# Gather of the experts' inputs one group ahead, sums in fixed bunches, and the norm's factors behind the gather

## Chip, cores and metric

One NeuronCore of a Trainium2 chip runs the whole program. The metric is the device time of one execution in microseconds. TensorE is written PE, VectorE DVE, ScalarE ACT, GpSimd POOL, and SyncE, which issues the loads, SP.

## What is computed

Three layers act on 512 tokens of 1024 numbers in float32: a hybrid layer, then two layers of a mixer followed by a mixture of experts. The change is in the two mixtures and in the norm before each:

```python
x = _layer_norm(DEEPNORM_ALPHA * x + mix, ln_g[i, 0], ln_b[i, 0])
ffn = _hierarchical_moe(x, ...)      # router: 4 groups, 8 experts each, top 2
x = _layer_norm(DEEPNORM_ALPHA * x + ffn, ln_g[i, 1], ln_b[i, 1])

def expert_block(xb, e):             # xb: the rows routed to expert e
    h = jax.nn.silu(xb @ w_gate[e]) * (xb @ w_up[e])
    return h @ w_down[e]
y = jax.ops.segment_sum(y_rows * row_gate[:, None], row_tok, num_segments=t + 1)[:t]
```

There are 32 experts with a hidden width of 512. The first mixer is a state-space scan (SSD), the second a dilated attention.

## The kernel before

The hybrid layer runs to about 1.3 ms, the SSD mixer to 1805 us. Then come the experts of layer 0, the attention, and the experts of layer 1.

**Experts (`moe`, from L2291).** Every expert has 64 slots; what does not fit goes to `moe_overflow`, a loop that runs zero times here. Two experts make a pair and lie side by side in PE's 128 columns: `experts_up` (L2127) and `experts_down` (L2160) issue each weight matmul as 64 columns at `tile_position=(0, 64 * u)`, `u` being the expert of the pair. 16 pairs run one after the other; the down matmuls of pair c - 1 stand behind the up matmuls of pair c. The weights are float32 and streamed: 6.29 MB an expert, 201.3 MB a layer, in 192 pieces of 1.05 MB, each of two loads of 512 KB from SP's queue (`mload`, L2097). A piece is the four k steps of one of gate or up for one expert, or half of its down matrix. 11 buffers hold pieces (seven slots with the halves `rawa` and `rawb`, two `mrawp`, two `mraw`), and 11 pieces are asked for before the stage begins.

**Gather (`gather`, L2253).** For four experts (a group, two pairs) a one-hot `OH` of 256 slots picks the tokens: 64 matmuls of `X` (the normed input in a high and a low part, `hl`, four token tiles `t`, eight feature blocks `k`) make `XG`. It is done for a group right before that group's first pair, the second half of it inside that pair (`yield` after k = 3). Its PSUM banks `acc`, two of them, are shared with the sums. ACT and DVE take turns in emptying them (L2274, L2276).

**Sums (`combine`, L2187).** For each token tile and half of the features, `cmb` adds the slots' outputs `yy` back by a one-hot `sel`, and DVE adds the bank into `x`. `Fill` deals these out, three steps behind the up matmuls and three behind the down matmuls of a pair. The last group is 32 matmuls behind the last weight.

**Route (`route_with`, L1930, to `moe_gates`).** While the mixer's output projection (`g_out`, L305) makes token tile t, the tile before it is transposed (`tp`), copied (`xt`, ACT and DVE in turn), multiplied with the router weights (`pl`), and DVE picks group and two experts in a dozen small instructions (L1970 to L1982, one-hots `oh`, their sum `O`). Then `ln_apply` or `ln_apply3` normalises `x`. In `moe`, ACT casts `x` to the high part of `X` and POOL subtracts to get the low part (L2327, L2328). `moe_slots` (L2004) turns all four `O` into slot numbers `pos` in one group of matmuls `pp`, which needs the last tile; the first one-hot, the first gather and the first weight matmul follow.

**What sets the order.** The program is written as one stream; a scheduler moves instructions on each engine by its own estimates of when operands and buffers come free, so the order on an engine differs from the order written.

## Time and profile before

| | |
|---|---|
| time, median of 3 runs | 3299.06 us (3298.2 to 3310.43) |
| the profiled execution: its time, its span | 3303.4 us, 3301.6 us |
| mean granted clock of PE | 0.970 |
| PE busy | 3130.1 us (95%), 15183 matmul records |
| DVE, ACT, POOL busy | 1484.8, 998.4, 736.9 us |
| DMA | 603.43 MB, mean 183 GB/s |

A row of a timeline has start, duration, engine, line, operation, output and inputs by name, tile sizes and the number of records that were joined; in brackets stands the idle time before it and what ended it. A float32 matmul leaves two records, one of a split (fp32r) operand one. In the waits, "A <- B: total, times, longest" is time in which A had nothing to do until B ended; SPq is the queue of loads. [...]

### The profile page before, as it was taken

What the parts mean: (1) busy time and instruction counts of PE and PEld (TensorE: products, weight loads), DVE (VectorE), ACT (ScalarE), POOL (GpSimd) and SP (SyncE); (2) the same over time, 40 slices, a digit from 0 to 9 for tenths busy, and PEclk for the clock granted to TensorE, in tenths of its full rate; (3) what the DMA queues carried; (4) which work ended last, traced back from release to release, by engine and by line L of the source; (5) the groups of instructions that cost most, each with busy time, mean ns of one, the idle gap of its engine ahead of it and who ended that gap; (6) DMA issues with size and microseconds to landing.
All of it is one profiled execution on the core that took longest, in us unless ns stands there. A gap on an engine that the chain in (4) does not pass through costs nothing. (4 is left out here: it accounts for less than half of the span.)

```text
span 3301.6 us, 40067 instructions
## 1 busy us (share of the span) xinstructions
PE 3130.1 (95%) x15183; PEld 2166.0 (66%) x15183; DVE 1484.8 (45%) x3035; ACT 998.4 (30%) x1866; POOL 736.9 (22%) x560
## 2 busy tenths in 40 slices
PE   8899998999999999999998899999999988999997
PEld 6678787887877888777877544444488874444443
DVE  5655766533244313488767322222444464222223
ACT  4434666642232223244423100000234431000011
POOL 3442323422342222123224100000164321000000
PEclk9999999999998999999999899999999988999999
DMA  5624121225342323233434799999822237999996
GB/s 164 139 91 114 41 65 38 82 86 161 120 138 64 102 90 94 66 103 99 118 93 153 286 388 358 361 363 355 313 65 64 65 105 291 392 357 363 366 350 250
DMA packets 294433, 603.43 MB, mean 183 GB/s; under 512 B 29392, under 2 KB 154764, under 8 KB 294204
## 3 DMA queue, kind: packets, MB, share of 16 engines
q1 hardware_dynamic: 294236, 600.82, 52.5%
q8 instruction: 122, 2.00, 0.2%
q14 instruction: 75, 0.61, 0.1%
HBM read 587.04 MB, written 13.70 MB: 182 GB/s over the span
## 5 line engine op out<-in xcount | busy, mean ns | idle before, releaser
L333 POOL TENSOR_TENSOR lob<-rawb,whi 128x1024 fp32r<-128x1024 f32 (+1 forms) x57 | 151.5, 2660 | 779.0 <-ACTq L2214 538.4
L352 PE MATMUL lin<-hT,whi 128*128 128x512 f32 (+1 forms) x912 | 302.5, 411 | 22.3 <-ACT g L538 13.8
L2134 PE MATMUL mm<-rawb,XG 128*64 128x512 f32 x704 | 262.1, 600 | 0.0
L263 PE MATMUL mm<-hT,whi 128*128 128x512 f32 x832 | 260.1, 394 | 0.0
L2134 PE MATMUL mm<-rawa,XG 128*64 128x512 f32 x704 | 259.1, 599 | 0.0
L243 DVE TENSOR_TENSOR loa<-rawa,whi 128x1024 fp32r<-128x1024 f32 (+2 forms) x90 | 111.9, 1243 | 281.5 <-ACT whi L242 280.1
L243 POOL TENSOR_TENSOR lob<-rawb,whi 128x1024 fp32r<-128x1024 f32 x52 | 131.8, 2535 | 411.5 <-ACT whi L242 367.3
L352 PEld LDWEIGHTS lin<-hT,whi 128*128 128x128 f32 (+1 forms) x912 | 174.5, 194 | 69.1 <-ACT g L538 15.1
L242 ACT ACTIVATE whi<-rawa 128x1024 fp32r<-128x1024 f32 (+2 forms) x90 | 90.4, 1004 | 348.1 <-issue 184.3
L2269 PEld LDWEIGHTS xg<-OH,X 128*128 128x128 f32 x1024 | 132.0, 194 | 78.1 <-issue 74.6
L263 PEld LDWEIGHTS mm<-hT,whi 128*128 128x128 f32 x832 | 157.1, 189 | 38.0 <-ACT hT L439 0.2
L2197 PE MATMUL cmb<-yy,sel 128*128 128x512 f32 x512 | 155.7, 427 | 11.8 <-ACT yy L2177 2.9
L352 PE MATMUL lin<-xT,whi 128*128 128x512 f32 x512 | 165.2, 400 | 0.0
L2197 PEld LDWEIGHTS cmb<-yy,sel 128*128 128x128 f32 x512 | 90.8, 192 | 108.6 <-issue 57.1
L2269 PE MATMUL xg<-OH,X 128*128 128x256 f32 x1024 | 152.1, 296 | 2.7 <-DVE OH L2259 2.7
L390 POOL TENSOR_TENSOR ln<-lnv,mhalf 128x1 f32<-128x1 f32 x16 | 13.4, 840 | 603.7 <-DVE lnv L388 600.2
L263 PE MATMUL mm<-xT,whi 128*128 128x512 f32 (+1 forms) x400 | 129.9, 405 | 1.2 <-ACT xT L439 1.2
L2171 PE MATMUL py<-rawa,H 128*64 128x512 f32 x288 | 129.9, 598 | 0.0
L2134 PEld LDWEIGHTS mm<-rawa,XG 128*64 128x64 f32 x704 | 70.3, 136 | 90.3 <-issue 84.3
L369 PE MATMUL lin<-whi,hT 128*128 128x256 f32 x640 | 126.1, 289 | 1.7 <-ACT gv L992 1.1
L2171 PE MATMUL py<-rawb,H 128*64 128x512 f32 x288 | 127.4, 598 | 0.0
L333 DVE TENSOR_TENSOR loa<-rawa,whi 128x1024 fp32r<-128x1024 f32 (+1 forms) x55 | 73.9, 1344 | 110.2 <-ACT whi L332 103.2
(609 smaller groups left out, 7166.2 us busy)
## 6 DMA issues: line engine op xcount, KB each, us to landing
rawa<-in_moe_w_up_dram SPq DMA_DIRECT2D x92, 512.0 KB, 8.8
rawb<-in_moe_w_up_dram SPq DMA_DIRECT2D x92, 512.0 KB, 10.1
rawa<-in_moe_w_gate_dram SPq DMA_DIRECT2D x84, 512.0 KB, 8.3
rawb<-in_moe_w_gate_dram SPq DMA_DIRECT2D x84, 512.0 KB, 9.7
rawa<-in_moe_w_down_dram SPq DMA_DIRECT2D x72, 512.0 KB, 9.4
rawb<-in_moe_w_down_dram SPq DMA_DIRECT2D x72, 512.0 KB, 10.1
mrawp<-in_moe_w_down_dram SPq DMA_DIRECT2D x60, 512.0 KB, 10.1
mraw<-in_moe_w_gate_dram SPq DMA_DIRECT2D x52, 512.0 KB, 9.1
```

What stands on the lines that cost most here:

```text
L242: nc.scalar.activation(h, t[:, :, :o], AF.Copy)
L243: (self.second if j else nc.vector).tensor_tensor(lo[:, :, :o], t[:, :, :o], h, op=OP.subtract)
L263: nc.tensor.matmul(ps[j][:m], lhsT=w[:, k, 128 * j:128 * j + m], rhs=v, start=(kc + k == 0 and i == 0), stop=(kc + k == K - 1 and i == 2))
L333: (nc.gpsimd if j or self.late > 0 else nc.vector).tensor_tensor(lo, t, h, op=OP.subtract)
L352: nc.tensor.matmul(ps[:m], lhsT=w[:, k, 128 * j:128 * j + m], rhs=v, start=(k == 0 and i == 0), stop=(k == 7 and i == 2))
L369: nc.tensor.matmul(ps[:, :width], lhsT=v[:, 128 * t:128 * t + 128], rhs=w[:, k, :width], start=(k == 0 and i == 0), stop=(k == 7 and i == 2))
L390: self.nc.gpsimd.tensor_tensor(r, v, self.half[:, :n], op=OP.pow)
L2134: nc.tensor.matmul(ps[64 * u:64 * u + 64], lhsT=XG(4 * h + k, u), rhs=w[u][k], start=(h == k == 0), stop=(h == 1 and k == 3), skip_group_c ...
L2171: nc.tensor.matmul(py[c][s], lhsT=H[:, 2 * h + k, s], rhs=w[u][2 * k + c], start=(h == k == 0), stop=(h == k == 1), skip_group_check=True, ...
L2197: nc.tensor.matmul(ps, lhsT=sel[rows, 128 * t:128 * t + 128], rhs=yy[rows, hl, s], start=(n == 0), stop=(n == 2 * len(group) - 1))
L2269: nc.tensor.matmul(s, lhsT=X2[t][:, hl, k], rhs=OH[:, t], start=(hl == t == 0), stop=(hl == 1 and t == 3))
```

## The change

- The norm before the experts is split. The gather takes (x - mean) x r, made by ACT with a stride (`lny`), cast by ACT and subtracted by DVE; the gain and bias are applied by ACT when a gathered block is emptied (`gathered`), eight instructions of 256 columns for a group. The norm of `x` itself (`norm_in`) is done on DVE during the first pair.
- Slots, positions and the first one-hots are made for each token tile (`tile_slots`), and the first gather (`gather0`) goes by token tile into four `mm` banks.
- Later gathers are made one group ahead. Gather steps and sums stand in `between`, called behind each of gate, up and down, and are dealt out at four of six such places in two pairs.
- In a pair the expert `u` = 1 comes first.
- The sums of pair 14 are a group of their own, so the last group is 16 matmuls. The rows of gain and bias for the last norm are loaded ahead of the last down matmuls.
- `xT`, `hT` and `X` lie in four more fixed slots; the router's weights are padded from 36 to 40 columns; `moe_setup` loads gain and bias once more in columns (four small loads).

```diff
 class Block2:
-    def ln_apply3(self, p, x, t, stats, g, b, y):
-        m = p.tile([128, 1], F, name="lnmr", bufs=4)
-        nc.gpsimd.tensor_tensor(m, nm, r, op=OP.mult)
-        nc.scalar.activation(y, x[:, t], AF.Identity, bias=m, scale=r)
-        nc.vector.tensor_tensor(y, y, g, op=OP.mult)
-        nc.gpsimd.tensor_tensor(x[:, t], y, b, op=OP.add)
...
     def route_with(self, units, x, i, sums, p, xt, junk, y):
+        self.X2 = [self.in_slot(f"X{i}_{t}", self.SLOTS + t, [128, 2, 8, 128], R) for t in range(4)]
...
             if n % 2 == 0 and n:
-                self.route_tile(x, i, n // 2 - 1, pl, st, p, rows, y)
+                self.route_tile(x, i, n // 2 - 1, pl, p, y)
+                if n > 2:
+                    self.tile_slots(n // 2 - 2, pl)
         self.router_half(x, i, 7, xt, pl)
-        self.route_tile(x, i, 3, pl, st, p, rows, y)
+        self.tile_slots(2, pl)
+        self.route_tile(x, i, 3, pl, p, y)
+        self.tile_slots(3, pl)
         self.moe_gates(p)
...
-        (nc.scalar.activation(v, ps.rearrange("p (k t) -> p k t", k=4), AF.Copy) if h
-         else nc.vector.tensor_copy(v, ps.rearrange("p (k t) -> p k t", k=4)))
+        nc.scalar.activation(v, ps.rearrange("p (k t) -> p k t", k=4), AF.Copy)
...
-        if t == 2:
-            self.ln_apply3(p, x, t, st[t], rows[:, 0], rows[:, 1], y[:, t % 2])
-        else:
-            self.ln_apply(x, t, st[t], rows[:, 0], rows[:, 1], y[:, t % 2])
+        m = p.tile([128, 1], F, name="lnmr", bufs=4)
+        tt(m, nm, r, op=OP.mult)
+        X, z = self.X2[t], y[:, t % 2].rearrange("p (k f) -> p k f", k=8)
+        nc.scalar.activation(z, x[:, t].rearrange("p (f k) -> p k f", k=8), AF.Identity, bias=m, scale=r)
+        nc.scalar.activation(X[:, 0], z, AF.Copy)
+        tt(X[:, 1], z, X[:, 0], op=OP.subtract)
+
+    def tile_slots(self, t, pl):
+        pp = pl[t][:, 64:96]
+        for u in range(t + 1):
+            nc.tensor.matmul(pp, lhsT=self.lt16[:, 0 if u == t else 1], rhs=self.O[:, u], start=(u == 0), stop=(u == t),
+                             skip_group_check=True)
+        nc.vector.scalar_tensor_tensor(self.pos[:, t], pp, 1.0, self.O[:, t], op0=OP.add, op1=OP.mult)
+        self.one_hot(t, 0)
...
     def experts_up(self, piece, XG, n=2, between=lambda: None):
...
                 for k in range(4):
-                    for u in range(n):
+                    for u in reversed(range(n)):
                         nc.tensor.matmul(ps[64 * u:64 * u + 64], lhsT=XG(4 * h + k, u), rhs=w[u][k],
...
-                if which == h == 0:
-                    between()
+            between()
...
-    def experts_down(self, piece, H, gate, n=2):
+    def experts_down(self, piece, H, gate, n=2, between=lambda: None):
...
-                    for u in range(n):
+                    for u in reversed(range(n)):
...
+        between()
         yy = self.myy.tile([128, 2, D], R, name="yy")
...
+    def gather0(self, i):
+        xg = self.mq.tile([128, 8, 256], F, name="XG", bufs=2)
+        ps = [self.mm() for _ in range(4)]
+        s = lambda k: ps[k // 2][:, 256 * (k % 2):256 * (k % 2) + 256]
+        for t in range(4):
+            for k in range(8):
+                for hl in range(2):
+                    nc.tensor.matmul(s(k), lhsT=self.X2[t][:, hl, k], rhs=self.OH[:, t], start=(t == hl == 0),
+                                     stop=(t == 3 and hl == 1), skip_group_check=True)
+        for k in range(8):
+            self.gathered(i, xg, k, s(k))
+        return xg
+
+    def gathered(self, i, xg, k, ps):
+        self.nc.scalar.activation(xg[:, k], ps, AF.Identity, bias=self.gcol[:, i, 1, k:k + 1], scale=self.gcol[:, i, 0, k:k + 1])
+
+    def gather(self, i, e, out):
...
-            if k % 2:
-                o = xg[:, k - 1:k + 1].rearrange("p k s -> p (k s)")
-                if k % 4 == 1:
-                    nc.scalar.activation(o, ps, AF.Copy)
-                else:
-                    nc.vector.tensor_copy(o, ps)
-            if k == 3:
-                yield xg
+            self.gathered(i, xg, k, s)
+            yield
+        self.slot_values(e)
+        yield
...
+    def norm_in(self, x, i):
+        rows, y = (self.myy.tile([128, 2, D], F, name=n, tag="yy") for n in ("lnin", "lniny"))
+        for n, v in enumerate(("ln_g_2", "ln_b_2")):
+            self.bc_row(rows[:, n], self.a[v][i, 0])
+        for t in range(4):
+            self.ln_apply(x, t, (self.lnst2[:, t, 0:1], self.lnst2[:, t, 1:2]), rows[:, 0], rows[:, 1], y[:, t % 2])
+            yield
...
-                for t in range(4):
-                    xv = x[:, t].rearrange("p (f k) -> p k f", k=8)
-                    nc.scalar.activation(X2[t][:, 0], xv, AF.Copy)
-                    nc.gpsimd.tensor_tensor(X2[t][:, 1], xv, X2[t][:, 0], op=OP.subtract)
-                self.moe_slots(r, p)
...
+                XG = {0: self.gather0(i)}
...
+                def between():
+                    n = beat[0] = beat[0] + 1
+                    if n == 1:
+                        self.slot_values(0)
+                        self.norm_start()
+                    if n < 5:
+                        nq.step(1)
+                        gq.step((1, 3, 2, 3)[n - 1])
+                    elif (n - 5) % 6 in (0, 2, 3, 5):
+                        gq.step(1)
+                        cq.step(2)
+                        gq.step(2)
...
                         if c % 2 == 0:
-                            rest = self.gather(2 * c, X2)
-                            XG = next(rest)
+                            gq.flush()
+                            if c < 14:
+                                gq.add(self.gather(i, 2 * c + 4, XG))
...
-                    elif c and c % 2 == 0:
-                        fill.add(self.combine(x, group, self.ALPHA if c == 2 else 1.0))
+                    elif c and (c % 2 == 0 or c == 15):
+                        cq.add(self.combine(x, group, self.ALPHA if c == 2 else 1.0))
                         group = []
```

**PE, in the middle of layer 0's experts.** `mm` are up matmuls, `py0` and `py1` down matmuls of the two halves of the features, `cmb` sums, `xg` the gather. Slot numbers stand behind `rawa` and `rawb`: of slots 2 and 3, 1 and 2 or 3 and 4 one holds a piece of the one expert and one of the other. Before:

```order
L2171 MATMUL py1_14944<-rawb_1_77,H_14871 64x512
L2134 MATMUL mm_15050<-rawa_3_87,XG_15013 64x512
L2134 MATMUL mm_15050<-rawa_2_81,XG_15013 64x512
L2134 MATMUL mm_15050<-rawa_3_87,XG_15013 64x512
L2134 MATMUL mm_15050<-rawb_2_83,XG_15013 64x512
L2197 MATMUL cmb_15273<-yy_14971,sel_14976 128x512
L2197 MATMUL cmb_15279<-yy_14971,sel_14976 128x512
L2197 MATMUL cmb_15273<-yy_14971,sel_14976 128x512
L2197 MATMUL cmb_15279<-yy_14971,sel_14976 128x512
L2134 MATMUL mm_15050<-rawb_3_89,XG_15013 64x512
L2134 MATMUL mm_15050<-rawb_2_83,XG_15013 64x512
L2134 MATMUL mm_15050<-rawb_3_89,XG_15013 64x512
```

With the change, the same stage:

```order
L2186 MATMUL py1_15189<-rawb_2_83,H_15097 64x512
L2186 MATMUL py1_15189<-rawb_1_77,H_15097 64x512
L2213 MATMUL cmb_15338<-yy_15256,sel_15261 128x512 x2
L2213 MATMUL cmb_15344<-yy_15256,sel_15261 128x512
L2150 MATMUL mm_15275<-rawa_4_93,XG_14805 64x512
L2150 MATMUL mm_15275<-rawa_3_87,XG_14805 64x512
L2150 MATMUL mm_15275<-rawa_4_93,XG_14805 64x512
L2150 MATMUL mm_15275<-rawa_3_87,XG_14805 64x512
L2213 MATMUL cmb_15344<-yy_15256,sel_15261 128x512
L2304 MATMUL xg_15350<-OHr_13622,X0_0_13626 128x256
L2304 MATMUL xg_15350<-OHr_13622,X0_1_13627 128x256
L2304 MATMUL xg_15350<-OHr_13622,X0_2_13628 128x256
```

Before, the stretch ends behind one matmul of `rawb_2`, whose partner in `rawb_3` comes behind four sums. With the change the stretches between other work hold an even number from the two slots in turn, and single gather blocks and sums stand between them.

**PE, from the last projection to the first gather, layer 0.** `tp` are transposes of `x`, `pl` the router's matmuls (and with the change the slots of one tile), `pp` the slots of all tiles. Before:

```order
L1959 MATMUL pl<-wr_7981,xt 128x36 x4
L1954 MATMUL tp<-c_61,x_7968 128x128 x4
L1959 MATMUL pl<-wr_7981,xt 128x36 x8
L2013 LDWEIGHTS lt_8032
L2013 MATMUL pp<-O,lt_8032 128x32
```

With the change:

```order
L1970 MATMUL pl<-wr_7978,xt 128x40 x4
L1966 MATMUL tp<-c_61,x_7965 128x128 x4
L2279 MATMUL mm<-OHr,X_0_13626 128x256 x9
L2007 LDWEIGHTS lt_8036
L2007 MATMUL pl<-O,lt_8036 128x32
L2279 MATMUL mm<-OHr,X_0_13626 128x256 x7
L2007 LDWEIGHTS lt_8036
L2007 MATMUL pl<-O,lt_8036 128x32
```

Before, the ten matmuls and the four of `pp` follow the last `pl`, and all 64 of the gather come behind them (32 of these behind the first weights). With the change the 16 gather matmuls of tile 0 stand ahead of the last two `pl`, and those of tiles 1 and 2 between the slots of later tiles.

**POOL before and DVE after, in the route of layer 0.** `X` is the low part of the gather's input. POOL before:

```order
L2328 TENSOR_TENSOR X_14000<-x_7968,X_14000 128x1024
L390 TENSOR_TENSOR ln<-lnv,mhalf 128x1
L1369 TENSOR_TENSOR lnmr<-lnm,ln 128x1
L2328 TENSOR_TENSOR X_14004<-x_7968,X_14004 128x1024
L1372 TENSOR_TENSOR x_7968<-lny,lnrows 128x1024
L2031 CAST val<-c_61 128x128
L2037 CAST val_14053<-c_61 128x4 x4
L390 TENSOR_TENSOR ln<-lnv,mhalf 128x1
```

DVE with the change:

```order
L1995 TENSOR_TENSOR lnmr<-lnst 128x1
L1989 MAX m_8026<-rw 128x8
L1990 MAX_INDEX rix<-m_8026,rw 128x8
L1562 SCALAR_TENSOR_TENSOR x_7965,lnsum<-x_7965,mm 128x512
L1991 TENSOR_TENSOR oh<-c_61,rix 128x64
L1993 TENSOR_TENSOR O<-oh 128x32
L1999 TENSOR_TENSOR X_2_13628<-lny,X_2_13628 128x1024
L1982 SCALAR_TENSOR_TENSOR rw<-br_7982,lnst,pl 128x40
L2009 SCALAR_TENSOR_TENSOR pos<-pl,O 128x32
L1983 SCALAR_TENSOR_TENSOR rL<-rw,lnst,br_7982 128x40
L2014 TENSOR_TENSOR OHr<-c_61,pos 128x256
```

The four subtracts of 128x1024 have gone from POOL to DVE, where they stand between the routes of two tiles; the slots and the one-hot of a tile stand among the instructions of the next.

## Rows read from the trace of the kernel before

**Rows 1.** Windows: us; busy PE, PEld, DVE, ACT, POOL; PEclk, DMA share, GB/s.

```profile
1820.00:1840.00 20.00, 12.39 (x74) 10.24 (x75) 11.16 (x41) 2.95 (x4) 6.20 (x10) 0.65 0.05 14
1850.00:2350.00 500.00, 493.89 (x2218) 216.99 (x2216) 120.30 (x255) 45.59 (x73) 0.00 (x0) 1.00 0.97 372
1860.00:1880.00 20.00, 20.00 (x114) 9.80 (x112) 3.39 (x5) 3.65 (x6) 0.00 (x0) 1.00 1.03 413
2320.00:2340.00 20.00, 19.65 (x80) 8.12 (x79) 5.53 (x8) 1.97 (x3) 0.00 (x0) 1.00 1.03 410
2800.00:3200.00 400.00, 395.30 (x1752) 173.38 (x1749) 93.46 (x194) 35.72 (x57) 0.00 (x0) 1.00 0.96 370
```

**Rows 2.** Waits, expert stage of layer 0: total us, times, longest.

```profile
PEld mm L2134 <- DMA rawb<-in_moe_w_down_dram: 1.3, 4, 0.4
...
SPq L2097 <- PE mm L2134: 138.4, 109, 7.9
SPq L2097 <- PE py L2171: 66.5, 35, 7.2
```

**Rows 3.** PE's timeline in layer 0: start, us, engine, line, operation, tiles, records.

```profile
2137.90 1.94 PE L2134 MATMUL mm<-mraw,XG 128*64 128x512 f32 x8
2139.77 1.80 PE L2269 MATMUL xg<-OH,X 128*128 128x256 f32 x13
...
2145.86 1.93 PE L2171 MATMUL py<-rawa,H 128*64 128x512 f32 x4
2147.72 0.97 PE L2197 MATMUL cmb<-yy,sel 128*128 128x512 f32 x3
...
2165.12 1.07 PE L2134 MATMUL mm<-mrawp,XG 128*64 128x512 f32 x2
```

**Rows 4.** PE's timeline from the last projection to the first weight, layer 0.

```profile
1804.30 0.40 PE L305 MATMUL mm<-whi,ssd_yl 128*128 128x512 f32 x1
...
1814.73 3.63 PE L1959 MATMUL pl<-wr,xt 128*128 128x36 f32 x16 [5.94 <-DVE xt L1957]
...
1826.49 0.18 PE L2013 MATMUL pp<-O,lt 128*128 128x32 bf16 x1 [5.08 <-DVE O L1982]
...
1828.18 6.74 PE L2269 MATMUL xg<-OH,X 128*128 128x256 f32 x32 [1.39 <-DVE OH L2259]
...
1835.64 1.94 PE L2134 MATMUL mm<-rawa,XG 128*64 128x512 f32 x8
```

**Rows 5.** The timelines of DVE, then POOL, then ACT, same stretch.

```profile
1806.81 5.17 DVE L1981 TENSOR_TENSOR oh<-c,rix 128x32 f32<-128x32 f32 x2
...
1812.66 1.28 DVE L1361 SCALAR_TENSOR_TENSOR lny<-x,lnm,lnrows 128x1024 f32<-128x1024 f32 x1
...
1823.29 2.72 DVE L1997 TENSOR_TENSOR rex<-m 128x4 f32<-128x4 f32 x1
...
1827.62 1.77 DVE L2259 TENSOR_TENSOR OH<-c,pos 128x256 fp32r<-128x256 f32 x4
...
1806.79 2.85 POOL L2328 TENSOR_TENSOR X<-x,X 128x1024 fp32r<-128x1024 f32 x1 [3.36 <-DVE x L1569]
...
1823.14 2.85 POOL L2328 TENSOR_TENSOR X<-x,X 128x1024 fp32r<-128x1024 f32 x1 [3.79 <-ACT X L2327]
...
1804.61 2.10 ACT L2327 ACTIVATE X<-x 128x1024 fp32r<-128x1024 f32 x1
```

**Rows 6.** PE's timeline from the last projection to the first weight, layer 1.

```profile
2719.96 0.40 PE L305 MATMUL mm<-whi,mol 128*128 128x512 f32 x1
...
2745.28 1.94 PE L2134 MATMUL mm<-rawa,XG 128*64 128x512 f32 x8
```

**Rows 7.** PE's timeline at the end of layer 0's experts.

```profile
2377.20 2.13 PE L2197 MATMUL cmb<-yy,sel 128*128 128x512 f32 x8 [0.68 <-DVE x L2201]
```

**Rows 8.** ACT's timeline, layer 0's route and first gather.

```profile
1822.97 0.20 ACT L1995 ACTIVATE rg<-rg 128x16 f32<-128x16 f32 x1
...
1832.69 0.60 ACT L2274 ACTIVATE XG<-xg 128x512 f32<-128x512 f32 x1 [6.45 <-PE xg L2269]
```

More of the change, by code (lines that the diff above doesn't have):

```diff
@@ L1246, in block1 @@
         with ExitStack() as s1:
-            hp = self.pool(s1, "hT")
-            hT = [hp.tile([128, 8, 512], R, name=f"hT{i}") for i in range(2)]
+            hT = self.stage_in("hT")
             x = lambda k: (hT[0][:, k], hT[1][:, k])
@@ L1344, with ln_stats @@
     ALPHA = 4.0 ** 0.25
-    def ln_stats(self, p, x, t, sums, j):
+    def ln_stats(self, p, x, t, sums, j, out=(None, None)):
         nc = self.nc
-        nm = p.tile([128, 1], F, name="lnm", bufs=4)
+        nm = p.tile([128, 1], F, name="lnm", bufs=4) if out[0] is None else out[0]
         nc.vector.tensor_tensor(nm, sums[:, 0:1], sums[:, 1:2], op=OP.add)
@@ L1598, in ssd @@
                 fill.flush()
-            rows = q.tile([128, 2, D], F, name="lnrows", tag="xsT")
-            for n, v in enumerate((a["ln_g_2"][0, 0], a["ln_b_2"][0, 0])):
-                self.bc_row(rows[:, n], v)
             finish(3, y)
+            s1.close()
+            self.route_begin()
             xt = q.tile([128, 4, 512], F, name="xt", tag="xsT")
@@ L1606, in ssd @@
                             lambda t: q.tile([128, D], BF, name="lnj", tag="zt", bufs=1),
-                            rows, lny)
+                            lny)
 class Attn:
@@ L1644, in att_begin @@
     def att_begin(self, st):
-        xp = self.pool(st, "xT3")
-        self.xT = [xp.tile([128, 8, 512], R, name=f"xT{i}") for i in range(2)]
+        self.xT = self.stage_in("xTa")
         self.ap0 = self.pool(st, "att0", bufs=2)
@@ L1756, in att @@
                             lambda t: p2.tile([128, D], BF, name="lnj", tag="sS", bufs=4),
-                            rows, lny)
+                            lny)
     def att_qk(self, g, w, xx, cos, sin):
@@ L1919, in moe_setup @@
+                nc.vector.tensor_tensor(br[:, 1], br[:, 1], ps[:, 40:80], op=OP.add)
                 self.routers.append((wr, br))
         self.rL = p.tile([128, 4, 40], F, name="rL")
-        nc.gpsimd.memset(self.rL[:, :, 4:8], BIG)
         self.m8 = p.tile([128, 2, 4, 8], F, name="m8")
-        self.oh = [p.tile([128, 4, 32], F, name=f"oh{k}") for k in range(2)]
+        self.ohs = p.tile([128, 4, 2, 32], F, name="oh")
+        self.oh = [self.ohs[:, :, k] for k in range(2)]
         self.O = p.tile([128, 4, 32], BF, name="O")
@@ L1925, in moe_setup @@
         self.gate = [p.tile([128, 4], F, name=f"gate{k}") for k in range(2)]
+        self.gcol = p.tile([128, 2, 2, 8], F, name="gcol")
+        for i in range(2):
+            for n, v in enumerate(("ln_g_2", "ln_b_2")):
+                nc.sync.dma_start(self.gcol[:, i, n], a[v][i, 0].rearrange("(p k) -> p k", k=8))
         self.lt16 = p.tile([128, 2, 128], BF, name="lt16")
@@ L1928, in moe_setup, with route_begin, route_with @@
         nc.gpsimd.memset(self.lt16[:, 1], 1.0)
-    def route_with(self, units, x, i, sums, p, xt, junk, rows, y):
-        pl, v, st = {}, {}, {}
+    def route_begin(self):
+        self.rst = ExitStack()
+        p = self.pool(self.rst, "route", side="right")
+        self.pos = p.tile([128, 4, 32], F, name="pos")
+        self.OH = p.tile([128, 4, 256], R, name="OHr")
+        self.lnst = p.tile([128, 4, 2], F, name="lnst")
+    def route_with(self, units, x, i, sums, p, xt, junk, y):
+        self.X2 = [self.in_slot(f"X{i}_{t}", self.SLOTS + t, [128, 2, 8, 128], R) for t in range(4)]
+        pl = {}
         for n, _ in enumerate(units):
@@ L2002, in moe_gates @@
         nc.vector.tensor_tensor(g1, g0, ex, op=OP.mult)
-    def moe_slots(self, p, keep):
-        nc = self.nc
-        tt, stt = nc.vector.tensor_tensor, nc.vector.scalar_tensor_tensor
-        O, pos = self.O, self.pos
-        lt, one = self.lt16[:, 0], self.lt16[:, 1]
-        pp = self.acc("pp")
-        for t in range(4):
-            for u in range(t + 1):
-                nc.tensor.matmul(pp[:, 32 * t:32 * t + 32], lhsT=lt if u == t else one, rhs=O[:, u],
-                                 start=(u == 0), stop=(u == t))
-        for t in range(4):
-            nc.tensor.matmul(pp[:, 128:160], lhsT=one, rhs=O[:, t], start=(t == 0), stop=(t == 3))
-        stt(pos, pp[:, 0:128].rearrange("p (t e) -> p t e", t=4), 1.0, O, op0=OP.add, op1=OP.mult)
-        nc.vector.tensor_scalar(pos, pos, 1.0, None, op0=OP.subtract)
-        nc.vector.tensor_copy(self.cnt, pp[:, 128:160])
     def moe_values(self, p, keep):
@@ L2058, in moe_spill @@
         tt(st, end, nb, op=OP.subtract)
[L2059 removed]
+        ts(st, st, 64.0, -65.0, op0=OP.mult, op1=OP.add)
         far = 65536.0
```

161 lines of the change are left out of this document (86 added, 75 removed).

## Prediction

> **What bounds the kernel now.** I read the windows first, then the waits, then the timeline of TensorE (PE). In the two expert stages, which are 1060 of the 3301.6 us, PE is busy 99% of the time at full clock and the weight stream moves 372 and 370 GB/s, against 410 to 413 in its busiest stretches [rows 1]. The waits say who waits for whom: over 500 us PE waits 1.3 us for a weight, and the load queue (SPq) waits 138.4 and 66.5 us for buffers that PE has still to free [rows 2]. So PE sets the pace there, and the stream has some 10% in hand.
>
> What PE does with its time is in the timeline. A weight matmul fills 64 of the 128 columns, and each f32 instruction leaves two records. Eight records on alternating halves, four instructions, take 1.94 us; four records of one half, two instructions, take 1.93; one instruction by itself takes 1.07 [rows 3]. So an instruction holds its half for 1.93 - 1.07 = 0.86 us, and two on different halves overlap fully: with a partner it costs 0.43 us, and 0.86 if its partner comes only after other work.
>
> Between the mixers and the first weight matmul lies a second kind of time, PE idle. In layer 0 the last output-projection matmul starts at 1804.30 and the first weight matmul at 1835.64; between them PE waits 5.94 us for `xt` and 5.08 us for `O`, both from VectorE (DVE) [rows 4]. In that stretch PE runs the 32 gather matmuls in 6.74 us, with a mean granted clock of 0.65 [rows 1, 4]. DVE is late for small things: two 32-wide compares last 5.17 us and a 4-wide subtract 2.72 us, each while a 2.85 us subtract (or the add behind it) holds GpSimd (POOL) [rows 5]. In layer 1 the same path takes 25 us [rows 6].
>
> **Part 1: the order of the experts' matmuls.** I counted along PE's order, in the stretches of weight matmuls between other work, how many instructions have no partner on the other half: 74 of 768 in layer 0 and 76 in layer 1 before; 0 and 2 in the changed order. The reversed `u` does this, together with the bunches. Terms per layer: 74 x 0.43 = -31.8 us. Of the first group's gather 32 matmuls move out of the stage into the route; 13 of them take 1.80 us, so 32 take 4.4: -4.4. Of the sums 8 to 12 more matmuls fall before the last weight; three take 0.97 and eight 2.13 us [rows 3, 7], so 0.23 each and 0.27 for a start: +2.3. The sums stand in 8 to 11 more stretches: +2.5. Weight stretches fall only from 110 to 104 and 102, so the scheduler does not keep the "four bunches" as written: about -1, and gather stretches +1. The sum is -31.4. Walking the whole order with such prices gives 525 us before (measured 531) and 498 after in layer 0, 526 and 496 in layer 1, so -27 and -30. A denser PE leaves the stream less in hand: 189.8 MB after the prefetch over about 496 us is 383 GB/s, 93% of 410. I take 2 us off for loads that come late and put **-26 us a layer**; the bounds are -31 and, if the stream holds PE at today's 372 GB/s, 189.8/0.372 = 510 us, -21.
>
> What goes to other engines there: eight evacuations of 256 columns on ScalarE (ACT) per group replace two of 512 on ACT and two on DVE. No row shows 256; a 512-wide one takes 0.60 and a 16-wide 0.20 [rows 8]. Between them I take 0.45: 7 x 8 x 0.45 = 25 us, against 46 busy of 500 on ACT [rows 1]. The held-back norm is eight DVE instructions of 1.28 us [rows 5], where DVE is busy 120 of 500 [rows 1], and the first sum into `x` comes two pairs later. Both are hidden, and cost nothing as long as `XG` is a whole group ahead; if that cover were gone, 8 x 0.45 = 3.6 us a group would show, 25 us a layer.
>
> **Part 2: route to first weight.** POOL loses its four subtracts and the add of `ln_apply3`; DVE loses eight 1.28 us norm instructions and gets four subtracts; ACT gets all eight copies of `xt` and a strided `lny` for each tile (2.10 us, the price of the strided cast it replaces) beside a cast. Three tiles' slots, one-hots and gather matmuls now go ahead of the last tile's. What leaves the 31.3 us path of layer 0: the compares' 5.17 and the subtract's 2.72 us shrink to 0.3 and 0.2, as POOL holds nothing long any more, -7.4; two DVE norm instructions of 1.28 in front of the last tile's route, -2.6; three of four one-hots of the 1.77 us, -1.3 [rows 5]; 16 of 32 gather matmuls, -3.4 [rows 4]. Together -14.7. What comes in is on ACT: two copies of `xt` at 0.6 [rows 8], 1.2, and the tile before, whose `lny` 2.1 and cast (an estimate of 1.1, half of the strided one) stand ahead of the last tile's, 3.2. I count that once: -14.7 + 4.4 = -10.3, say **-10**; bounds -14.7, if ACT does it in its gaps, and -6, if it stands there twice. The last tile's own `lny`, cast and subtract, 4.5 us, run beside its route, slots and one-hot. Layer 1's path is 25.3 us [rows 6]; by layer 0's 21 it gains 4, by layer 0's difference 10; I take **-7**, with these as bounds.
>
> The queues: SP gets iota, gain and bias rows early, of some KB to 0.5 MB, beside 11 MB of prefetch that waits for PE anyway; the loads into `mraw` stand last in the prefetch, behind nothing that the first pair needs. The POOL queue only gets shorter. Four small loads and a few memsets in `moe_setup` lie under the first block: 0, at most +1.
>
> **Part 3: the ends.** After the last weight 20 to 24 sums remain for 32, 8 to 12 x 0.23 = 2 to 2.7 us [rows 7]; DVE's adds and norms follow in turn, so I take **-1.5** and **-2**. The loads of gain and bias now stand ahead of the last down matmuls, off that path.
>
> Sum: -52 - 17 - 3.5 = -72.5 us. The profiled execution took 3303.4, which gives 3231; the median of the runs, 3299.06, is 4.3 lower and gives 3227. I say 3229.
>
> **Rivals.** (B) *The weight stream becomes the bound.* For it: the mean is already 372 GB/s at a DMA share of 0.97, and a stage that is 5% shorter asks 383. Against it: 410 and 413 GB/s where it is full [rows 1], 205 us of SPq waiting for PE [rows 2], and 11 pieces of buffer. With 372 kept, -21 each and the ends lost: 3303 - 42 - 17 = 3244; if only half of the stages' gain comes, 3303 - 26 - 20 = 3257.
>
> [...]
>
> (C) *Slower: banks.* Gather and sums share two `acc` banks, and each bank of the gather is now emptied by two ACT instructions that queue behind ACT's other work, while more stretches follow one another. There are some 96 bank allocations a layer (28 gather, 64 and more sums). Waits of this kind exist: 0.68 us before the last sums [rows 7]. At 73/192 = 0.38 us each the gain is gone; at 0.5 the time is 3229 + 96 = 3325. Against it: ACT is idle 90% of the stage, and in the order the eight matmuls of a bank are mostly followed by weight matmuls, which use other banks.
>
> (D) *The balance does not pay*, because the halves overlap less than the rows of the timeline make me think, or the later piece, now asked for first, is awaited each time. Only routes and ends remain: 3303 - 20 = 3283, or 3279 by the median. Against it: the rows of one half [rows 3] and that the walk with these prices gives 525 of the measured 531.
>
> **How the numbers follow.** A measurement of this kernel tells 0.5%, 16.5 us. Forecast (3206 to 3240) 0.60; B (3240 to 3262) 0.18; D (3270 to 3290) 0.10; C or another new wait, 0.06; a larger gain, if the stage's 5 us of small waits vanish too, -31 - 5 a layer, -15 and -10 in the routes: 3299 - 72 - 25 - 4 = 3198, below 3206 then, 0.06. The range takes the forecast and B to where D begins: 3206 to 3266. Faster by over 0.5% are forecast, B, the larger gain and half of D: 0.89; within 0.5%: the other half of D and a little of C: 0.07; slower: 0.04.
>
> **What would show it.** In the profile after: expert stages of about 505 us at 390 GB/s or so, with PE still 97% busy or more and hardly a weight awaited (B: PE's weight loads wait for DMA, SPq no longer for PE); weight stretches of eight records in 1.94 us or of multiples; the first weight about 21 us after the last projection in both layers, no DVE compare of 5 us; no idle on PE behind the ACT line of `gathered` (C); PE total lower by some 50 us. A stage of 520 us or more with PE busy throughout would make the reading of the halves wrong; idle PE before weight matmuls would make the 10% in hand wrong.

## The result and the profile after

The changed kernel takes 3212.53 us (median of 4 runs, 3209.83 to 3224.15), the kernel before 3301.26 beside it (3298.2 to 3310.43): a ratio of 0.9726, 95% interval 0.971 to 0.9742, or 88.7 us less. It was forecast at 3229 (3206 to 3266). The span of the profiled execution is 3211.0 us, 90.6 less than before.

The timeline of PE cuts that span at four kinds of row: the start of the last projection matmul, of the first and the last weight matmul of a layer, and the end. The table has these cuts for every kernel that was run. "Route" is from the last projection to the first weight, "stage" from the first weight to the last, "between" from layer 0's last weight to the attention's last projection, "rest" the whole way from the first matmul of the SSD mixer's output projection to the end. The last column is the median of the runs and its ratio to the kernel before on the same chip. All in us.

| kernel | route 0 | stage 0 | between | route 1 | stage 1 | end | rest | time, ratio (interval) |
|---|---|---|---|---|---|---|---|---|
| before | 31.3 | 530.5 | 353.8 | 25.3 | 530.1 | 26.3 | 1752.2 | 3301.3 |
| changed | 16.1 | 502.8 | 353.8 | 14.9 | 497.4 | 28.8 | 1667.5 | 3212.5, 0.9726 (0.971 to 0.9742) |
| changed again (e10) | 16.1 | 499.5 | 354.4 | 14.9 | 499.1 | 28.8 | 1666.9 | 3212.9, 0.9727 (0.9711 to 0.9743) |
| e1 before, order reversed | 30.7 | 496.6 | 356.8 | 26.7 | 496.5 | 26.2 | 1686.9 | 3234.5, 0.9792 (0.9778 to 0.9806) |
| e2 changed, order forward | 16.1 | 535.9 | 353.3 | 14.9 | 533.8 | 26.0 | 1735.1 | 3283.3, 0.9935 (0.9921 to 0.9948) |
| e3 low part on POOL | 17.6 | 501.8 | 353.3 | 16.5 | 500.1 | 27.0 | 1669.4 | 3220.8, 0.9743 (0.9729 to 0.9757) |
| e4 last sums together | 16.0 | 495.3 | 358.3 | 14.9 | 496.2 | 25.1 | 1657.9 | 3211.4, 0.9717 (0.9704 to 0.9731) |
| e5 slots at once | 22.0 | 504.0 | 354.5 | 21.5 | 502.7 | 27.0 | 1685.2 | 3234.4, 0.9798 (0.9783 to 0.9812) |
| e6 two thirds of the stream | 16.1 | 489.9 | 359.8 | 14.9 | 489.9 | 30.7 | 1653.0 | 3204.3, 0.9708 (0.969 to 0.9725) |
| e7 old dealing | 16.1 | 499.9 | 353.5 | 15.0 | 497.2 | 28.8 | 1663.3 | 3212.4, 0.9728 (0.9714 to 0.9742) |
| e8 old dealing, last together | 16.1 | 494.0 | 357.9 | 14.9 | 494.2 | 25.5 | 1659.9 | 3205.9, 0.971 (0.9696 to 0.9724) |
| e9 reversed, POOL relieved | 28.5 | 496.5 | 359.1 | 25.0 | 496.6 | 25.4 | 1683.5 | 3237.6, 0.9796 (0.9778 to 0.9813) |
| e11 as e8, again | 16.1 | 495.7 | 361.1 | 14.9 | 494.2 | 25.4 | 1660.9 | 3209.6, 0.9704 (0.9687 to 0.9722) |
| e12 norm in the route | 27.1 | 501.7 | 355.4 | 23.9 | 498.8 | 27.0 | 1685.4 | 3236.2, 0.979 (0.9772 to 0.9807) |

So the 90.6 us are 60.4 in the two stages, 25.6 in the two routes, nothing between, 2.5 the wrong way at the end. The remaining 7.1 us lie ahead of the last projection of layer 0, 5.9 of them ahead of that mixer's first output matmul, and those can't be put down to the change. Between 300 and 580 us the granted clock (PEclk, as a share of full speed) was 0.94 in one profile and 0.98 in the other, and over all the kernels it lies at 0.92 to 0.98 there, with either code (0.98 in e1, which is the kernel before up to the experts). That is why "rest" is the better column for small differences.

The windows of the changed kernel (columns as in [rows 1]) answer to the windows of before:

```profile
1800.00:1850.00 50.00, 47.86 (x284) 26.87 (x283) 24.48 (x73) 14.23 (x24) 3.32 (x10) 1.00 0.98 377
1820.00:2310.00 490.00, 479.84 (x2294) 208.56 (x2292) 129.06 (x276) 72.36 (x120) 1.09 (x1) 0.99 1.00 390
2010.00:2022.00 12.00, 10.41 (x40) 4.27 (x38) 2.58 (x13) 0.60 (x1) 0.00 (x0) 0.72 1.03 409
2700.00:3170.00 470.00, 461.05 (x2224) 202.65 (x2226) 117.94 (x264) 68.45 (x115) 0.00 (x0) 1.00 1.01 396
```

PE is still 98% busy, the stream now moves 390 and 396 GB/s, and ACT has 72 busy us where it had 46. The waits of the changed kernel in layer 0's stage:

```profile
PE tp L2170 <- DVE hid L2167: 5.9, 5, 1.2
PE xg L2304 <- ACT XG L2287: 1.5, 2, 0.8
...
PEld mm L2150 <- DMA mrawp<-in_moe_w_down_dram: 0.9, 3, 0.4
...
SPq L2114 <- PE mm L2150: 140.8, 81, 6.2
SPq L2114 <- PE py L2186: 67.6, 34, 6.4
```

The load queue waits for PE as long as before [rows 2], so the stream still isn't the bound. PE's largest wait, the one for `hid`, isn't new: over the whole stage it is 5.9 us here, 4.0 in the kernel before, and 5.9 in e1. The timeline in the middle of the stage answers to [rows 3]:

```profile
1961.96 1.09 PE L2213 MATMUL cmb<-yy,sel 128*128 128x512 f32 x4
1962.99 1.94 PE L2150 MATMUL mm<-rawa,XG 128*64 128x512 f32 x8
1964.85 1.23 PE L2304 MATMUL xg<-OHr,X 128*128 128x256 f32 x8
1965.92 1.10 PE L2213 MATMUL cmb<-yy,sel 128*128 128x512 f32 x4
1966.95 1.94 PE L2150 MATMUL mm<-rawb,XG 128*64 128x512 f32 x8
```

No weight row stands here with a lone pair of records; each stretch is eight records in 1.94 us. Counted over the stage of layer 0, 44 of 110 stretches of weight rows had an odd number of instructions before, and none of 104 has now (2 of 102 in layer 1). The route's last rows answer to [rows 4] and [rows 6], layer 0 first:

```profile
1797.13 0.39 PE L309 MATMUL mm<-whi,ssd_yl 128*128 128x512 f32 x1
...
1811.19 2.15 PE L2279 MATMUL mm<-OHr,X 128*128 128x256 f32 x16 [1.01 <-DVE OHr L2014]
1813.28 1.94 PE L2150 MATMUL mm<-rawa,XG 128*64 128x512 f32 x8
...
2669.85 0.39 PE L309 MATMUL mm<-whi,mol 128*128 128x512 f32 x1
...
2682.73 2.14 PE L2279 MATMUL mm<-OHr,X 128*128 128x256 f32 x16 [0.89 <-DVE OHr L2014]
2684.80 1.94 PE L2150 MATMUL mm<-rawa,XG 128*64 128x512 f32 x8
```

The longest idle time left in layer 0 is 1.01 us, and 16 gather matmuls take 2.15 us where 32 took 6.74: the granted clock is 1.00 between 1800 and 1850 us, where before it was 0.65 between 1820 and 1840 [rows 1], with waits of 5.94 and 5.08 us [rows 4].

### The profile page after: what moved, and what is told of

The parts are those of the page before. It is cut to its first block, busy times and chain, and to the rows that moved or that the text cites. A ratio compares the mean times of both kernels' runs of the same rounds, so it can differ in the third digit from the quotient of the medians.

```text
span 3211.0 us, 40168 instructions
## 1 busy us (share of the span) xinstructions
PE 3053.2 (95%) x15183; PEld 2117.8 (66%) x15183; DVE 1464.2 (46%) x3019; ACT 1061.7 (33%) x1976; POOL 699.3 (22%) x551
## 5 line engine op out<-in xcount | busy, mean ns | idle before, releaser
L356 PEld LDWEIGHTS lin<-hT,whi 128*128 128x128 f32 (+1 forms) x912 | 173.5, 193 | 68.2 <-ACT g L542 14.9
L2150 PE MATMUL mm<-rawa,XG 128*64 128x512 f32 x704 | 193.1, 599 | 0.0
L2150 PE MATMUL mm<-rawb,XG 128*64 128x512 f32 x704 | 192.2, 599 | 0.0
L2287 ACT ACTIVATE XG<-xg,gcol 128x256 f32<-128x256 f32 x112 | 62.3, 563 | 349.9 <-PE xg L2304 258.9
L356 PE MATMUL lin<-xTa,whi 128*128 128x512 f32 x512 | 165.6, 401 | 0.0
L2304 PEld LDWEIGHTS xg<-OHr,X 128*128 128x128 f32 x896 | 114.8, 188 | 68.1 <-issue 42.2
L2220 DVE TENSOR_TENSOR x<-x,cmb 128x512 f32<-128x512 f32 x112 | 75.7, 684 | 135.5 <-PE cmb L2213 135.4
L2304 PE MATMUL xg<-OHr,X 128*128 128x256 f32 x896 | 132.8, 291 | 3.8 <-ACT XG L2287 3.0
L267 PE MATMUL mm<-xTs,whi 128*128 128x512 f32 (+1 forms) x400 | 129.0, 402 | 0.0
L394 POOL TENSOR_TENSOR ln<-lnv,mhalf 128x1 f32<-128x1 f32 x8 | 6.5, 806 | 534.8 <-DVE lnv L392 527.2
L2194 DVE SCALAR_TENSOR_TENSOR yy<-py,gt,yy 128x512 fp32r<-128x512 f32 x64 | 48.0, 750 | 160.2 <-ACT yy L2193 157.3
```

The costliest lines, as they stand in the source:

```text
L267: nc.tensor.matmul(ps[j][:m], lhsT=w[:, k, 128 * j:128 * j + m], rhs=v, start=(kc + k == 0 and i == 0), stop=(kc + k == K - 1 and i == 2))
L356: nc.tensor.matmul(ps[:m], lhsT=w[:, k, 128 * j:128 * j + m], rhs=v, start=(k == 0 and i == 0), stop=(k == 7 and i == 2))
L2150: nc.tensor.matmul(ps[64 * u:64 * u + 64], lhsT=XG(4 * h + k, u), rhs=w[u][k], start=(h == k == 0), stop=(h == 1 and k == 3), skip_group_c ...
L2194: nc.vector.scalar_tensor_tensor(yy[r, 1, s], py[c][r], gate, yy[r, 0, s], op0=OP.mult, op1=OP.subtract)
L2220: nc.vector.tensor_tensor(x[:, t, s], x[:, t, s], ps, op=OP.add)
L2287: self.nc.scalar.activation(xg[:, k], ps, AF.Identity, bias=self.gcol[:, i, 1, k:k + 1], scale=self.gcol[:, i, 0, k:k + 1])
```

## Experiments

**e1 and e2: the order of the two experts.** e1 is the kernel before with one word in two loops, e2 the changed kernel without it:

```diff
-                    for u in range(n):
+                    for u in reversed(range(n)):
```

> The kernel before with one edit: of a pair of experts the second one's matmul comes first, in the up and the down matmuls; nothing else of the change. Theory H (halves): this order alone leaves no matmul without its partner; in the order of PE 2 of 768 are unpaired in either layer, where there were 74 and 76. A walk along that order with the prices of the prediction gives 491 us a stage where it gave 525 and 526 before, so the stages fall by 34 us each and the time from 3301 to about 3233; route and ends stay as they were (31.3 and 25.3 us from the last projection to the first weight). Theory G (group ahead and bunches): the unpaired matmuls come from a gather that stands right ahead of its pair, and the order of the two experts matters little: 3290 to 3305. Theory B (stream): PE has no longer the say at 189.8 MB in 483 us, 393 GB/s; weights are awaited and the stages stop at 500 or more: 3250 or more.

> The changed kernel with the first expert's matmul first again, all else as changed. Theory H: 76 and 74 matmuls are unpaired again, the walk gives 533 us a stage where it gave 498 and 496, so +35 and +37: about 3285, and the gather ahead and the bunches by themselves are worth nothing, even 7 us a stage less than nothing against the 525 of the kernel before. Theory G: within 15 us of 3212. The route stays at 16 and 15 us in both.

e1 took 3234.5 us, stages 496.6 and 496.5; e2 took 3283.3, stages 535.9 and 533.8. Theory H said 3233 and 3285. The reversed order alone is worth 34 us a stage, more than the whole change is there (28 and 33; 31 in both of e10); without it the changed stages are 4 to 5 us longer than before. Theory G falls. Counted as above, e1 has 2 odd stretches a layer and e2 has 50; from start to start the weight rows of layer 0 take 352.2 us in e1 for 383.8 before, 31.6 us less, or 0.44 for each of the 72 that found a partner. The rows of e2 show the lone instructions back:

```profile
2014.19 1.02 PE L2150 MATMUL mm<-rawa,XG 128*64 128x512 f32 x2
2015.14 1.21 PE L2304 MATMUL xg<-OHr,X 128*128 128x256 f32 x8
2016.28 1.50 PE L2186 MATMUL py<-rawb,H 128*64 128x512 f32 x3
```

Theory B falls for e1 as well: its windows have the stream at 396 GB/s over 470 us, and PE keeps its pace.

```profile
1840.00:2310.00 470.00, 462.07 (x2226) 203.38 (x2224) 122.62 (x265) 45.76 (x73) 0.00 (x0) 1.00 1.01 396
```

**e7, e8, e11: the dealing of gather and sums.** e7 takes the bunches away from the changed kernel; e8, and e11 once more, also join the last sums as in e4 below.

```diff
-                        gq.step((1, 3, 2, 3)[n - 1])
-                    elif (n - 5) % 6 in (0, 2, 3, 5):
-                        gq.step(1)
-                        cq.step(2)
-                        gq.step(2)
+                    if n <= 2:
+                        gq.step((5, 4)[n - 1])
+                    elif n > 4 and (n - 5) % 6 in (0, 3):
+                        gq.step(5)
+                    if n > 4 and (n - 5) % 3 != 2:
+                        cq.step(3)
```

> The changed kernel with gather and sums dealt out in larger lumps, as before: half a gather behind each up matrix of gate in a pair, three sums behind gate and three behind up, nothing behind the down matmuls; the gather still a group ahead, the order of the two experts as changed. Theory L2 (switches): each switch of PE between weights, gather and sums costs 0.15 to 0.3 us; the walk gives 492.9 and 491.0 us for 497.9 and 495.7, so -5 each and about 3202. Theory G: the four bunches are right and fewer places make PE wait for banks: 3212 or more. Theory B: at 395 GB/s the stream stops the gain, stages stay at 500 and 497: 3212.

> As the old dealing, and with the sums of pairs 14 and 15 as one last group of 32 and the last norm's rows loaded behind the loop. Theory L2: the walk gives 488.3 and 487.8, with the few us above the walk as before 491 to 493; 4.5 us more between the stages and 3.7 less at the end as seen with the last sums together: about 3197. Theory B: 189.8 MB in 480 us are 395 GB/s on the mean; if the stream holds PE there, the stages stop at 495 to 497: 3204 to 3208.

> The changed kernel with the old dealing and the last sums together once more, beside the changed kernel on one chip. If its lead is real (stages 494 for 503 and 497, the end 25.5 for 28.8, 4 us more between the stages): 5 to 8 us below the changed kernel. If it was the chip: within 3 us of it.

e7 is as fast as the change (0.9728 and 0.9726), 3 us and 0.2 shorter in the stages where the walk had said 5: theory L2 misses. The numbers of B and G come out, but the reason of neither shows: no PE row waits for a load in e7's stages, and PE's idle time in layer 0's is 8.7 us, against 10.2 in the changed kernel. Counted from start to start in layer 0's timeline, 61 stretches of sums take 68.9 us in the changed kernel and 52 take 68.8 in e7; 55 stretches of gather take 61.2, and so do 46. What a sum or a gather block costs beside its matmuls doesn't depend on how many stretches they are spread over, so where the bunches stand is worth nothing here. e8's stages, 494 us, lie between theories L2 and B, its time in B's range, again with no PE row that waits for a load. e8 and e11 are ahead of the changed kernel by 6 to 8 us in "rest" (1659.9 and 1660.9 for 1667.5 and 1666.9), by 0.2% in the ratio, with intervals that overlap; the lead of e11 over e10 on one chip was 3.2 us in the medians, short of the 5 to 8 that were to make it real. It is the best version found, by little; e4 has no smaller a lead in "rest", and none in the median.

**e4: the last sums in one group.**

```diff
-                        rows = self.myy.tile([128, 2, D], F, name="lnrows", tag="yy")
...
-                    elif c and (c % 2 == 0 or c == 15):
+                    elif c and (c % 2 == 0):
...
+                rows = self.myy.tile([128, 2, D], F, name="lnrows", tag="yy")
...
```

> The changed kernel with the sums of pairs 14 and 15 as one last group of 32 matmuls again (and the rows of gain and bias for the last norm loaded behind the loop, where they were before). As the prediction had it, the group of its own saves 2 us at each end and costs 2 to 4 in each stage: the end behind the last weight of layer 1 grows from 28.8 to 31 us, the stages shrink by 4: about 3208. Theory L: the adds of pair 14 behind the last weight are what PE waits for ahead of the last sums; together, the end is 26 us or less as before (26.3), the stages shrink by 4 each as the walk says (493 and 492 for 498 and 496): about 3202.

Theory L's end holds, 25.1 us. The stages are 7.5 and 1.2 us shorter than the changed kernel's, or 4.2 and 2.9 shorter than e10's, for 4 each. But "between" grew by 4.5, which it didn't have, and the way to the SSD mixer's output projection was 4.9 us longer in the profiled execution; the time is 3211.4 and not 3202. The end of layer 1, the changed kernel (PE, then a row of DVE) and then e4:

```profile
3180.93 1.89 PE L2186 MATMUL py<-rawb,H 128*64 128x512 f32 x8
3182.74 1.20 PE L2213 MATMUL cmb<-yy,sel 128*128 128x512 f32 x4
3184.26 0.74 PE L2213 MATMUL cmb<-yy,sel 128*128 128x512 f32 x2 [0.31 <-DVE x L2220]
3185.51 0.72 PE L2213 MATMUL cmb<-yy,sel 128*128 128x512 f32 x2 [0.52 <-DVE x L2220]
3187.86 3.80 PE L2213 MATMUL cmb<-yy,sel 128*128 128x512 f32 x8 [1.63 <-DVEq L2230]
...
3186.27 0.69 DVE L2220 TENSOR_TENSOR x<-x,cmb 128x512 f32<-128x512 f32 x1 [0.22 <-PE cmb L2213]
```

```profile
3179.86 1.89 PE L2186 MATMUL py<-rawb,H 128*64 128x512 f32 x8
3183.82 5.17 PE L2213 MATMUL cmb<-yy,sel 128*128 128x512 f32 x20 [2.08 <-DVEq L2230]
```

The overflow loop (L2230) stands between pair 14's sums and the last ones, and DVE reaches it only after pair 14's adds, the last of which ends at 3186.96: the last sums begin 5.0 us behind the last weights' end in place of 2.1.

**e5, e3, e9, e12: the parts of the route.** e5 makes the slots of all tiles at once; e3 gives the low part back to POOL; e9 is e1 with POOL's five large instructions on DVE; e12 puts the norm of `x` back into the route.

```diff
...
-        self.tile_slots(2, pl)
         self.route_tile(x, i, 3, pl, p, y)
-        self.tile_slots(3, pl)
+        pp = self.tp("pp")
...
+        for t in range(4):
+            self.one_hot(t, 0)
```

```diff
-        tt(X[:, 1], z, X[:, 0], op=OP.subtract)
+        nc.gpsimd.tensor_tensor(X[:, 1], z, X[:, 0], op=OP.subtract)
```

```diff
-        nc.gpsimd.tensor_tensor(x[:, t], y, b, op=OP.add)
+        nc.vector.tensor_tensor(x[:, t], y, b, op=OP.add)
...
-                    nc.gpsimd.tensor_tensor(X2[t][:, 1], xv, X2[t][:, 0], op=OP.subtract)
+                    nc.vector.tensor_tensor(X2[t][:, 1], xv, X2[t][:, 0], op=OP.subtract)
```

```diff
...
         tt(X[:, 1], z, X[:, 0], op=OP.subtract)
+        self.ln_apply(x, t, (nm, r), self.nrows[:, 0], self.nrows[:, 1], y[:, t % 2])
...
-                nq.add(self.norm_in(x, i))
```

> The changed kernel with the slots of all four token tiles in one group of matmuls behind the last tile's route again, and the four first one-hots behind them; the split of the norm, the low part on DVE and all else stay. Theory T: slots and gather by token tile gave the route its gain, since 48 of the 64 gather matmuls ran in gaps; now all 64 stand behind the last one-hot, 48 x 0.13 = 6.3 us more, and a little for the group: the first weight 22 to 24 us behind the last projection in place of 16.1 and 14.9, the time 3224 to 3228. Theory N: the norm split off the gather's path and POOL relieved gave it: 17 to 18 us, 3213 to 3218.

> The changed kernel with the subtract that makes the low part of the gather's input on POOL again, all else as changed. Theory P (POOL's long subtracts hold up DVE's small instructions): DVE shows compares and adds of 2 to 5 us again while POOL subtracts, and the first weight comes 3 to 6 us later in each layer than the 16.1 and 14.9 us behind the last projection: 3218 to 3225. Theory T (slots and gather by token tile gave the route's gain): only the last tile's subtract is on the path, 2.85 for 1.23 us, so at most 1.6 us a layer: 3212 to 3216, and no stretched DVE rows.

> The kernel before with the reversed order of the two experts, and with POOL's four subtracts for the low part and its add in the norm given to DVE; slots, gather and norm stay where they were. Theory P (POOL's long instructions stretch DVE's small ones): the rows of 2.3 to 3 us are gone, the first weight comes 3 to 6 us earlier than the 30.7 and 26.7 us behind the last projection with the reversed order alone, though DVE has 4 x 1.25 us more to do: 3223 to 3229 where the reversed order alone took 3234. Theory N: the rows go, and DVE's own work takes their place: 30 and 26 us, 3232 to 3238.

> The changed kernel with the norm of x itself back in the route (two DVE instructions of 1.28 us behind each tile's subtract, rows of gain and bias loaded where they were before) and no norm in the first pair; slots and gather by token tile and the gain behind the gather as changed. Theory D (DVE's own large instructions were what its small ones stood behind): of the route's gain of 15.2 and 10.4 us the slots by tile gave 5.9 and 6.6 and the low part on DVE 1.5 and 1.6; the rest, 7.8 and 2.2, is the norm held back, so the first weight comes 22 to 24 and 17 us behind the last projection, time 3220 to 3224. Theory A: the last tiles' DVE work fits beside ACT's lny and cast, and the rest came from elsewhere (the norm no longer ahead of the gather's input): at most 18 and 16 us, 3213 to 3216.

e5: the routes grow by 5.9 and 6.6 us, theory T (its time was above the range, since the stages grew by 1 to 5 too and the way to the SSD mixer's output projection by 3.6). The row that pays is one stretch of all 64 gather matmuls behind the last one-hot:

```profile
1812.57 9.35 PE L2284 MATMUL mm<-OHr,X 128*128 128x256 f32 x64 [0.84 <-DVE OHr L2019]
```

e3: the routes grow by 1.5 and 1.6, theory T's number, though DVE's rows are stretched as theory P says (two 40-wide instructions take 2.04 and 2.15 us, where the changed kernel has 0.26). (Its time of 3220.8 would fit P, but "rest" is 1.9 us longer than in the changed kernel; the other 6 lie ahead of the SSD mixer's output projection.) DVE, then POOL:

```profile
1802.28 2.04 DVE L1983 SCALAR_TENSOR_TENSOR rL<-rw,lnst,br 128x40 f32<-128x40 f32 x1
...
1801.89 2.37 POOL L1999 TENSOR_TENSOR X<-lny,X 128x1024 fp32r<-128x1024 f32 x1 [3.92 <-ACT X L1998]
```

The 40-wide DVE instruction ends at 1804.32, 0.06 us after POOL's. The second one ends at 1814.14, and POOL's last subtract at 1814.09. The rows show that they end together, not what holds DVE.

Theory T's reason, a longer subtract on the path, isn't what the rows of PE show. In layer 0 its clock is 0.61 for 3.6 us, behind a wait of 0.97 us for DVE; in layer 1 it waits 1.54 and 1.03 us for DVE, and the last 16 gather matmuls take 3.48 us, where the changed kernel has 2.14. The window of layer 0 and PE's timeline in layer 1:

```profile
1811.40:1815.00 3.60, 3.60 (x22) 3.42 (x21) 3.23 (x9) 0.46 (x2) 2.37 (x1) 0.61 1.05 416
```

```profile
2687.23 0.18 PE L2007 MATMUL pl<-O,lt 128*128 128x32 bf16 x1 [1.54 <-DVE O L1993]
2688.43 3.48 PE L2279 MATMUL mm<-OHr,X 128*128 128x256 f32 x16 [1.03 <-DVE OHr L2014]
```

e9: the long compares go (two take 0.29 us, where e1 has 2.96), but the routes shrink by 2.2 and 1.7 only, between theories P and N; DVE is now busy with POOL's work:

```profile
1809.25 2.02 DVE L2328 TENSOR_TENSOR X<-x,X 128x1024 fp32r<-128x1024 f32 x1
...
1815.79 2.00 DVE L2328 TENSOR_TENSOR X<-x,X 128x1024 fp32r<-128x1024 f32 x1
...
1819.20 1.27 DVE L1362 SCALAR_TENSOR_TENSOR x<-lny,ln,lnrows 128x1024 f32<-128x1024 f32 x1
```

e12: the routes grow by 11.0 and 9.0 us, more than theory D's 7.8 and 2.2, and theory A falls. A norm instruction of DVE stands ahead of a tile's positions, PE waits 1.89 us for these, and the granted clock is 0.74 between 1800 and 1840 us: 16 gather matmuls take 3.78 us. So the 11.0 us are waits and a lower clock together. DVE's timeline, the window, and PE's timeline:

```profile
1805.58 1.28 DVE L1364 SCALAR_TENSOR_TENSOR lny<-x,lnst,lnrows 128x1024 f32<-128x1024 f32 x1
...
1807.56 0.19 DVE L2018 SCALAR_TENSOR_TENSOR pos<-pl,O 128x32 f32<-128x32 f32 x1
```

```profile
1800.00:1840.00 40.00, 35.64 (x186) 28.21 (x186) 22.17 (x95) 14.38 (x21) 3.39 (x10) 0.74 0.71 247
```

```profile
1807.79 1.09 PE L1974 MATMUL tp<-c,x 128*128 128x128 f32 x4 [1.89 <-DVE pos L2018]
...
1823.98 3.78 PE L2288 MATMUL mm<-OHr,X 128*128 128x256 f32 x16 [0.30 <-DVE OHr L2023]
```

Undone one at a time, slots (5.9), low part (1.5) and held-back norm (11.0) add up to 18.4 us in layer 0, where the route gained 15.2, and to 17.2 in layer 1, where it gained 10.4: a part loses some of its worth without the others. One cost that they share is the clock: between 1800 and 1823 us it is 0.78 in e5 (eight records of `pl` take 0.98 us there, the next eight 1.93), and 0.74 between 1800 and 1840 in e12, where the changed kernel has 1.00. Not undone by itself were the copies of `xt`, which ACT alone makes now, and the smaller number of DVE's small instructions for a tile.

**e6: a lighter stream.** The kernel leaves out part of the weights, so its result is another.

```diff
+            if j and n < len(self.order) and self.mcount > 11:
+                continue
```

> The changed kernel that leaves out the second 512 KB load of each piece in the seven slots after the first eleven pieces, so the stream of a layer is about a third smaller and these weights are stale. PE's order moves with it: the walk gives 498 us a stage (498 and 496 for the changed kernel). Theory PE: the stream hides nearly wholly already; the 4.9 and 1.7 us by which the measured stages (502.8, 497.4) pass the walk are DVE's and ACT's handovers and stay: 500 to 503. Theory B: they are late weights at 390 to 396 GB/s and go: 498 and 498, and the changed kernel could lose no more PE time without paying it to the stream.

The stages took 489.9 us each, under both theories. The window shows PE without its waits, at 267 GB/s:

```profile
1820.00:2310.00 490.00, 488.45 (x2322) 213.86 (x2318) 135.33 (x285) 75.75 (x124) 5.31 (x2) 1.00 0.76 267
```

But PE's order moved with the loads. The transposes of `hid` no longer wait. In layer 0's stage 24 of 91 stretches of weight rows have an odd number of instructions again, and 224 matmuls of sums stand in it for 236, in 46 stretches and 59.6 us for 61 and 68.9. The run can't tell the stream from the order, and stays inconclusive on what the last 10% of the stream cost.

**e10: the changed kernel again.**

> The changed kernel itself, on the same chip as the two others: 0.9726 of the kernel before by the runs at hand, 3209 to 3216. Route 16 and 15 us, stages 497 to 503, the first block up to 6 us longer or shorter by the granted clock alone (0.94 or 0.98 between 300 and 580 us).

It repeats the result, 0.9727, with stages of 499.5 and 499.1.

## Why the prediction was right, and where it wasn't

The profiled execution became 90.6 us shorter where 72.5 were forecast. Of the 18.1 us more, 8.4 are the stages' and 8.6 the routes'; the ends cost 6.0 against the forecast, and 7.1 us ahead of the last projection, which no term had, make up for these by luck.

**What bounds the stages: right.** An unpaired matmul was priced at 0.43 us and costs 0.44 by e1's weight rows; e1 and e2 move each stage by 74 to 76 of them in both directions, within 3 us of the walk's differences. 396 GB/s is the mean over 470 us in the changed kernel, and the best 20 us before are 413 [rows 1].

**The -26 us a layer: too small.** Measured were -27.7 and -32.7, and -31.0 in both stages of e10. The 2 us taken off for late loads didn't occur: the longest sum of waits for one kind of weight is 0.9 us. "Together with the bunches" was wrong: the order does it alone, and what the rest of the change does in the stages costs 1 to 6 us against e1. The terms +2.5, +1 and -1 for starts of stretches have no support either, as e7 shows. Counted from start to start in layer 0 of e10, weight rows give -30.4 (forecast -31.8), the gather -4.6 (-4.4), the sums +2.5 (+2.3, and +2.5 for starts), and the other small matmuls +1.5, which no term had. That -31.4 came so near to -31.0 is in part luck.

**ACT's evacuations: right.** They take 0.56 us and not 0.45, 31 us in all, and PE waits 1.5 us for them (rival C). Rival D is refuted by e1 and e2.

**The routes: right in sign, too small, and for the wrong reason.** Measured were -15.2 and -10.4 for -10 and -7, a little beyond the bounds of -14.7 and -10. The step that failed is "the compares' 5.17 and the subtract's 2.72 us shrink ..., -7.4": with POOL relieved the stretched rows go, and the routes gain 2 us (e9; e3 loses 1.5 the other way), since DVE's new work takes their place. The 2.6 us for two norm instructions were mis-sized: held back, the norm is worth 11.0 and 9.0 (e12). One-hots and gather, 4.7, measured 5.9 and 6.6 (e5), and the gather that is left ran at 0.13 us a matmul, not at 0.21, with the clock at 1.00. The +4.4 for ACT wasn't paid as it was worked out: the `lny` and cast of the tile before end at 1796.02, ahead of the last projection at 1797.13. But that the last tile's own `lny`, cast and subtract "run beside its route" is wrong. DVE's order has the subtract ahead of that route, and DVE waits for ACT's cast:

```profile
1803.06 1.95 PE L1970 MATMUL pl<-wr,xt 128*128 128x40 f32 x16 [0.49 <-DVE m L1989]
...
1805.90 1.23 DVE L1999 TENSOR_TENSOR X<-lny,X 128x1024 fp32r<-128x1024 f32 x1 [1.86 <-ACT X L1998]
1807.04 0.25 DVE L1982 SCALAR_TENSOR_TENSOR rw<-br,lnst,pl 128x40 f32<-128x40 f32 x1
```

The last router matmul ends at 1805.01 and the route of its tile begins at 1807.04 (2676.64 and 2678.70 in layer 1). PE fills part of these 2 us with another tile's gather and stands idle for 0.24, 0.41 and 1.01 us behind it, so up to 1.7 us are still to be won there.

**The ends: wrong.** -1.5 and -2 were forecast; it is 0 between the layers and +2.5 at the end. At the end, the step "DVE's adds and norms follow in turn" left out that the overflow loop holds PE until DVE has passed pair 14's adds (e4). Between the layers e4 is 4.5 us longer than the changed kernel, so the group of its own saves time there; why the stretch is still as long as before stays open.
